# A feed-forward block's up-projections in pairs, by seven products of half size

## The chip, the cores and the metric

The kernel runs on one core of a Trainium2 chip. The metric is device microseconds of one execution: the median of three runs is 2164.41 us (2162.79 to 2165.35). TensorE (PE) multiplies into eight PSUM banks; VectorE (DVE), ScalarE (ACT) and GpSimd (POOL) do the elementwise work; SyncE (SP) issues the transfers.

## The reference, cut to what matters

One decoder layer on x of 1024 tokens by 1024 channels, all in float32: four token mixers, a cross-attention, and the feed-forward block. Each ends in `x <- LayerNorm(ALPHA * x + y)`. What is touched is the last:

```python
def _swiglu(x, w1, w3, w2):          # w1, w3: 1024 x 2816, w2: 2816 x 1024
    return (jax.nn.silu(x @ w1) * (x @ w3)) @ w2
x = _layer_norm(ALPHA * x + _swiglu(x, w1, w3, w2), ln_g[2], ln_b[2])
```

## The kernel before

**Products in three passes.** Every float32 operand is split into a high part (rounded, a copy on ACT) and a low part (the rest, a subtraction, on DVE or POOL): `split`, L153. A product is then three matmuls (`mm3`, L165): high by high for all slices of the sum, then low by high and high by low. `weight` (L157) loads 128 x 1024 numbers (512 KB) and splits them; raw, high and low tiles have two buffers each.

**The feed-forward stage.** The stream lies transposed: eight tiles x2 of 128 channels by 1024 tokens. The 2816 hidden channels are 22 blocks of 128. Of a block, `ffn_up` (L1427) makes w1 and w3 products for a half of 512 tokens: 24 matmuls each of 128x512 (8 slices of the sum, three passes). silu (ACT), the product with the w3 result (DVE) and a split give the tiles hh and hl. `ffn_down` (L1445) multiplies one block's 128 hidden channels by w2 for 8 output tiles and 2 halves: 3 matmuls into a PSUM bank, and one DVE addition into x2, 16 per block (L1459).

**Order.** The program is written out in one order; a scheduler then fixes each engine's own order from it, and each engine works its list in that order. First (LEAD = 3) blocks 0 to 2 for the first half of the tokens, while `Norm.steps` of the layer norm before runs for the second half beside them; `sink2` (L1407) splits each finished tile into the x2A (first half) or x2B (second half) operands, and POOL scales x2 by ALPHA. Then blocks 2 to 0 for the second half, their down-projections, and blocks 3 to 17 one by one, up and down in turn. The last four blocks (TAIL = 4) go by slices of 512, 256 and 256 tokens: all four blocks up, then down for that slice, weights loaded anew for each. A slice's norm (`Norm`: sum over eight tiles, mean matmul ps_mean, eight centred squares and their sum lnq, variance matmul ps_vc, a short DVE/ACT chain, broadcast matmul ps_rs, eight multiplications and affine steps) is laid beside the next slice's products; its matmuls stand at fixed places in PE's list (`queued`, L181). `LastNorm` does the last slice's.

Of the kernel before, what the change touches and what calls it, by code (L numbers as in the profile page):

```python
# [54 lines left out]
for _name, _w in (("ident", 128), ("bones", 128), ("ones256", 128), ("ones1k", 128), ("gce", 256),  # L55
                  ("tri", 128), ("id2", 64), ("ce", 256)):
    CC[_name] = _n
    _n += _w
# [34 lines left out]
def hybrid_kernel(ctx, tc, io, out):  # L93
# [12 lines left out]
    stg = ctx.enter_context(tc.tile_pool(name="stg", bufs=3))  # L106
    dp = ctx.enter_context(tc.tile_pool(name="dp", bufs=1, space=DRAM))
# [28 lines left out]
    def load_consts():  # L136
        nc.sync.dma_start(cst, io["consts"][:, 0:CC["ce"]])
# [1158 lines left out]

    def attend(hf, h):

        def scores(i):
# [6 lines left out]
            pr = t4.tile([P, MEM], F32, tag="xp", name="xp", bufs=2)  # L1306
# [114 lines left out]

    hid = {}

    def ffn_weights(f, e1=nc.vector, e3=nc.vector, **kw):
        return weight(io["ffn_w1"][f], eng=e1, **kw), weight(io["ffn_w3"][f], eng=e3)

    def ffn_up(f, sls, ws, steps=(0, 0)):  # L1427

        if f not in hid:
            hid[f] = tuple(pM.tile([P, T], F32R, tag="M", name=n) for n in ("hh", "hl"))  # L1430
        hh, hl = hid[f]
        for sl in sls:
            hf, n = sl.start // TH, sl.stop - sl.start
# [11 lines left out]
    def ffn_down(fs, ws, sls, ln=None):  # L1445
# [7 lines left out]
        for j0 in range(0, KD, 2):  # L1453
# [153 lines left out]
```

## Time and profile before

| what | value |
|---|---|
| median of three runs | 2164.41 us |
| the profiled execution | 2169.53 us, span 2167.4 us |
| granted TensorE clock, mean | 0.986 |
| PE busy | 2127.2 us (98%) |
| DVE / ACT / POOL busy | 1148.7 (53%) / 724.2 (33%) / 210.2 us (10%) |
| DMA | 161.12 MB, mean 74 GB/s |
| feed-forward stage | 1388.8 us to the end |

The page shows PE as busy nearly throughout, in matmuls that overlap (one of 128x512 is shown as 0.39 us, though the next begins 0.23 us later). So the busy share is no measure of the rate: count matmuls in a stretch instead. The windows of the rows below cut the stage at its own borders: the first blocks, the long middle, and three slices.

### The profile page before, as it was taken

To read this page: it belongs to the slowest core of one execution; us is meant where nothing else is said; L and a number is where in the kernel's file an instruction comes from. 1 tells how busy PE (TensorE), PEld (TensorE's weight loads), DVE (VectorE), ACT (ScalarE), POOL (GpSimd) and SP (SyncE) were. 2 spreads that over 40 slices of the span, in tenths; PEclk is the share of its full clock that TensorE was granted. 3 is DMA by queue.
4 is the path that set the end of the run, shared out by engine and by line. 5 is a ranking of instruction groups with operands and counts; after the bars stand their busy time and mean duration, and the time that the engine had idled before them with its cause. 6 is when DMAs were issued, how large, how long until landed. Compare 5 with 4: busy or idle time off the path is not lost. (4 is left out here: it accounts for less than half of the span.)

```text
span 2167.4 us, 29103 instructions
## 1 busy us (share of the span) xinstructions
PE 2127.2 (98%) x11884; PEld 1746.4 (81%) x11884; DVE 1148.7 (53%) x2028; ACT 724.2 (33%) x1163; POOL 210.2 (10%) x173
## 2 busy tenths in 40 slices
PE   9999999999999999999999999999999999999997
PEld 7877877787888888888897888778888888888787
DVE  5365498434544343334575446755554544545577
ACT  3243212266466564223243333331111111111224
POOL 0000000000001111211032000440000000000122
PEclk9999999999999999999999999999999999999999
DMA  6123221223211111113342112321111111111411
GB/s 212 49 70 88 72 87 61 88 78 102 76 61 60 49 52 47 53 47 109 111 160 97 31 58 88 127 65 52 59 49 39 59 49 40 59 49 59 146 69 49
DMA packets 87684, 161.12 MB, mean 74 GB/s; under 512 B 19606, under 2 KB 43848, under 8 KB 87552
## 3 DMA queue, kind: packets, MB, share of 16 engines
q1 hardware_dynamic: 87552, 159.28, 22.8%
q8 instruction: 93, 1.52, 0.3%
q14 instruction: 39, 0.32, 0.0%
HBM read 134.50 MB, written 24.76 MB: 73 GB/s over the span
## 5 line engine op out<-in xcount | busy, mean ns | idle before, releaser
L154 ACT CAST whi<-wraw 128x1024 fp32r<-128x1024 f32 x189 | 198.0, 1049 | 336.8 <-issue 192.8
L155 DVE TENSOR_TENSOR wlo<-wraw,whi 128x1024 fp32r<-128x1024 f32 x164 | 215.2, 1313 | 167.6 <-ACT whi L154 167.5
L176 PE MATMUL ps_gate<-xl,whi 128*128 128x512 f32 x512 | 201.5, 394 | 0.0
L175 PE MATMUL ps_gate<-xh,wlo 128*128 128x512 f32 x512 | 201.3, 393 | 0.0
L1459 DVE TENSOR_TENSOR x<-x,ps_w 128x512 f32<-128x512 f32 (+1 forms) x306 | 189.1, 673 | 11.8 <-PE ps_w L176 11.4
L172 PE MATMUL ps_gate<-xh,whi 128*128 128x512 f32 x512 | 165.6, 402 | 0.0
L175 PE MATMUL ps_g<-xh,wlo 128*128 128x512 f32 x400 | 157.8, 395 | 0.0
L176 PE MATMUL ps_g<-xl,whi 128*128 128x512 f32 x400 | 157.7, 394 | 0.0
L175 PE MATMUL ps_w<-x2B,wlo 128*128 128x512 f32 (+1 forms) x416 | 147.5, 365 | 3.6 <-POOL wlo L155 3.5
L176 PE MATMUL ps_w<-x2B,whi 128*128 128x512 f32 (+1 forms) x416 | 147.1, 364 | 0.0
L176 PE MATMUL ps_w<-hl,whi 128*128 128x512 f32 (+1 forms) x384 | 141.5, 374 | 1.9 <-DVE hl L155 1.7
L172 PE MATMUL ps_g<-xh,whi 128*128 128x512 f32 x400 | 140.4, 416 | 2.2 <-ACT xh L154 2.2
L175 PE MATMUL ps_w<-hh,wlo 128*128 128x512 f32 (+1 forms) x384 | 141.2, 373 | 0.0
L155 POOL TENSOR_TENSOR wlo<-wraw,whi 128x1024 fp32r<-128x1024 f32 x25 | 63.2, 2530 | 778.3 <-ACT whi L154 772.3
L175 PE MATMUL ps_w<-x2A,wlo 128*128 128x512 f32 x352 | 137.4, 390 | 0.0
L176 PE MATMUL ps_w<-x2A,whi 128*128 128x512 f32 x352 | 137.2, 390 | 0.0
L172 PE MATMUL ps_w<-hh,whi 128*128 128x512 f32 (+1 forms) x384 | 134.2, 375 | 2.1 <-ACT hh L154 2.1
L1442 DVE TENSOR_TENSOR hs<-hs,ps_w 128x512 f32<-128x512 f32 (+1 forms) x48 | 30.8, 642 | 177.5 <-PE ps_w L176 177.3
L176 PEld LDWEIGHTS ps_gate<-xl,whi 128*128 128x128 f32 x512 | 96.8, 189 | 20.7 <-issue 0.2
L175 PEld LDWEIGHTS ps_gate<-xh,wlo 128*128 128x128 f32 x512 | 96.7, 189 | 20.6 <-issue 0.2
L172 PEld LDWEIGHTS ps_gate<-xh,whi 128*128 128x128 f32 x512 | 94.7, 190 | 19.4 <-issue 1.9
L1050 POOL TENSOR_TENSOR merged<-merged,gsig 128x512 f32<-128x512 f32 x48 | 66.5, 1385 | 399.2 <-DVE gsig L1049 289.5
(457 smaller groups left out, 4259.6 us busy)
## 6 DMA issues: line engine op xcount, KB each, us to landing
wraw<-ffn_w SPq DMA_DIRECT2D x84, 512.0 KB
wraw<-wblk SPq DMA_DIRECT2D x57, 512.0 KB
wraw<-xa_wo SPq DMA_DIRECT2D x16, 512.0 KB
xraw<-xT SPq DMA_DIRECT2D x16, 256.0 KB
yld<-y_d SPq DMA_DIRECT2D x16, 256.0 KB
uraw<-ups SPq DMA_DIRECT2D x32, 128.0 KB
wraw<-w_out SPq DMA_DIRECT2D x8, 512.0 KB
xr<-xT SPq DMA_DIRECT2D x16, 256.0 KB
```

The source lines that it names most:

```text
L154: nc.scalar.copy(hi, src)
L155: eng.tensor_tensor(out=lo, in0=src, in1=hi.bitcast(F32), op=ALU.subtract)
L172: mm(ps, lhsT=pairs[i][0], rhs=pairs[i][2], start=start and i == 0, stop=False)
L175: mm(ps, lhsT=ll, rhs=rh, start=False, stop=False)
L176: latest[0] = mm(ps, lhsT=lh, rhs=rl, start=False, stop=stop and i == n + min(lag, n) - 1)
L1050: nc.gpsimd.tensor_tensor(out=mj, in0=mj, in1=sg, op=ALU.add)
L1442: tt(out=s, in0=s, in1=p[1], op=ALU.mult)
L1459: tt(out=x2[j][:, sl], in0=x2[j][:, sl], in1=ps, op=ALU.add)
```

## The change

Blocks 0 to 3 (LEAD = 4) are made as before, for one half at a time. Blocks 4 to 21 are taken as nine pairs. For a pair, w1 is a matrix of 256 by 1024: two block rows by two halves of the sum; x is two halves of the channels by two halves of the tokens. The product of two 2 x 2 block matrices takes eight half-sized products, or, by Strassen's scheme in Winograd's form, seven, of sums of blocks. `seven` (new) does this for w1 and then for w3: each of seven products is 12 matmuls of 128x512 (4 slices, three passes), against 96 matmuls for the same part before; four weight sums (POOL, `comb`), and seven sums of results (DVE). The sums of x are made once: eight in `sink2`, on POOL, beside the first blocks (xT12, xT3), and xT4 after them. Weights come as pieces of 128 x 2 x 512 (high and low together), each split by ACT and DVE, kept in a ring of five (`top_up`); raw rows are loaded one unit ahead. `down` sums a pair's two blocks in PSUM (6 matmuls, 8 DVE additions per block); the ALPHA scaling goes into the first of these additions. The last four blocks' slices (and of blocks 16 and 17 the second half's) hold only down-projections, with six w2 rows kept in SBUF; the norms of the first two slices add their sums on POOL instead of DVE. Constants that later stages don't need get a pool that closes before the last stages, which gives two more buffers.

```diff
     def sink2(hf):
         def f(j, ap):
             split(xf[hf].h[j], xf[hf].l[j], ap)
-            nc.gpsimd.tensor_scalar(out=ap, in0=ap, scalar1=ALPHA, scalar2=0.0, op0=ALU.mult, op1=ALU.add)
+            if hf == 1 and j >= KD // 2:
+                if not xt:
+                    xt.extend((HL(pA, "A", "xT12"), HL(t4, "T", "xT3", KD // 2)))
+                k = j - KD // 2
+                b11, b12 = (x2[k][:, hs(i)] for i in range(2))
+                t1 = diff(b12, b11)
+                split(xt[0].h[k], xt[0].l[k], t1)
+                t2 = diff(ap, t1)
+                split(xt[0].h[j], xt[0].l[j], t2)
+                t3 = diff(ap, b12)
+                split(xt[1].h[k], xt[1].l[k], t3)
...
-    LEAD, TAIL = 3, 4
+    LEAD = 4
...
+    RING = ((pB, "B"), (wp, "whi"), (wp, "wlo"), (wp, "whi"), (wp, "wlo"))
...
+    def sums(raws):
+        a11, a21, a22 = raws[0][:, 0:TH], raws[1][:, 0:TH], raws[1][:, TH:]
+        s1 = comb(a21, a22, ALU.add)
+        s2 = comb(s1, a11, ALU.subtract)
+        return s1, s2, comb(a11, a21, ALU.subtract)
...
+            s1, s2, s3 = ss
+            a = [r[:, i * TH:(i + 1) * TH] for r in raws for i in range(2)]
+            yield piece(a[0])
+            if more:
+                nxt = rows(units[u + 1], u + 1)
+            for src in (a[1], s2, s1, s3, a[3]):
+                yield piece(src)
+            s4 = comb(a[1], s2, ALU.subtract)
+            t = piece(s4)
+            ss = sums(nxt) if more and units[u + 1][0] != "ffn_w2" else None
+            yield t
...
+    def down(f, hfs, first=False):
+        for jh in range(2):
+            top_up(1)
+            w = made[used[0]:used[0] + 2]
+            for j in range(HK):
+                cs = slice(j * P, (j + 1) * P)
+                for hf in hfs:
+                    ps = gps("ps_w2")
+                    mm3(ps, [(w[i][:, 0, cs], w[i][:, 1, cs], hid[f + i, hf][:, 0], hid[f + i, hf][:, 1])
+                             for i in range(2)])
...
+        def product(n):
+            top_up()
+            ps = alloc()
+            w, (h, l) = made[used[0]], b[n]
+            mm3(ps, [(w[:, 0, k * P:(k + 1) * P], w[:, 1, k * P:(k + 1) * P], h[k], l[k]) for k in range(HK)])
+            used[0] += 1
...
+        u = term()
+        nc.scalar.copy(u, product(0))
+        done(0, 0, u, product(1))
+        tt(out=u, in0=u, in1=product(2), op=ALU.add)
+        v = term()
+        tt(out=v, in0=u, in1=product(3), op=ALU.add)
+        ps = product(4)
+        tt(out=u, in0=u, in1=ps, op=ALU.add)
+        done(1, 1, v, ps)
+        done(1, 0, u, product(5))
+        done(0, 1, v, product(6))
...
+        def hidden(i, l, a, ps):
+            x = t4.tile([P, TH], F32, tag="xp", name="hs", bufs=1)
+            tt(out=x, in0=a, in1=ps, op=ALU.add)
+            tt(out=x, in0=x, in1=gate[i, l], op=ALU.mult)
+            t = hid_tile(f + i, l, *((t4, "T") if lastp else ()))
+            split(t[:, 0], t[:, 1], x)
+
+        seven(lambda: sps("ps_w1"), rhs, gate_of)
+        if LEAD < f < NFF - 2:
+            down(f - 2, (0,) if f == NFF - 4 else (0, 1))
...
+        seven(lambda: gps("ps_w3"), rhs, hidden, keep)
...
+        ln = Norm(x2, sl, 2, gps, nc.gpsimd) if n < 2 else LastNorm(x2, sl, 2, gps)
```

What stands where, first on POOL in the first blocks (x2 tiles 0 to 7 end in 18 to 25 before and in 25 to 32 after; wlo is a weight's low part, the last two those of block 3). Before, behind the second half's multiplications:

```order
L1136 TENSOR_SCALAR x2_9718<-x2_9718,par_80 128x512
L1136 TENSOR_SCALAR x2_9719<-x2_9719,par_80 128x512
L1136 TENSOR_SCALAR x2_9720<-x2_9720,par_80 128x512
L1410 TENSOR_SCALAR x2_9718<-x2_9718 128x512
L1410 TENSOR_SCALAR x2_9719<-x2_9719 128x512
L1136 TENSOR_SCALAR x2_9721<-x2_9721,par_80 128x512
L1410 TENSOR_SCALAR x2_9720<-x2_9720 128x512
L1136 TENSOR_SCALAR x2_9722<-x2_9722,par_80 128x512
L1410 TENSOR_SCALAR x2_9721<-x2_9721 128x512
```

After:

```order
L1422 TENSOR_TENSOR xdiff_11849<-x2_9729,x2_9725 128x512
L1144 TENSOR_SCALAR x2_9730<-x2_9730,par_84 128x512
L162 TENSOR_TENSOR wlo_11910<-wraw_11907,whi_11909 128x1024
L1144 TENSOR_SCALAR x2_9731<-x2_9731,par_84 128x512
L1144 TENSOR_SCALAR x2_9732<-x2_9732,par_84 128x512
L1422 TENSOR_TENSOR xdiff_11857<-x2_9726 128x512
L1422 TENSOR_TENSOR xdiff_11861<-x2_9730,xdiff_11857 128x512
L1422 TENSOR_TENSOR xdiff_11865<-x2_9730,x2_9726 128x512
L1422 TENSOR_TENSOR xdiff_11873<-x2_9727 128x512
L1422 TENSOR_TENSOR xdiff_11877<-x2_9731,xdiff_11873 128x512
L1422 TENSOR_TENSOR xdiff_11881<-x2_9731,x2_9727 128x512
L162 TENSOR_TENSOR wlo_11916<-wraw_11913,whi_11915 128x1024
```

Short scalings of one input have given way to differences of two inputs, and the low parts of a fourth block's weights, 1024 wide, now stand among and behind them.

Second, on DVE in the middle. Before, where one block's up-projection ends and its predecessor's down-projection begins (hl is a hidden tile's low part):

```order
L155 TENSOR_TENSOR wlo_14059<-wraw_14056,whi_14058 128x1024
L1442 TENSOR_TENSOR hs_14051<-hs_14051,ps_w3_14026 128x512
L1459 TENSOR_TENSOR x2_9718<-x2_9718,ps_w2_14062 128x512
L155 TENSOR_TENSOR wlo_14145<-wraw_14142,whi_14144 128x1024
L155 TENSOR_TENSOR hl_13945<-hs_14051,hh_13944 128x512
L1459 TENSOR_TENSOR x2_9718<-x2_9718,ps_w2_14063 128x512
L1459 TENSOR_TENSOR x2_9719<-x2_9719,ps_w2_14064 128x512
```

After, in the w3 part of a pair, behind the fifth of its seven products (piece is a weight piece's low part, hid a hidden tile's):

```order
L1594 TENSOR_TENSOR term_13580<-term_13580,ps_w3_13673 128x512
L1654 TENSOR_TENSOR hs_13687<-term_13648,ps_w3_13673 128x512
L162 TENSOR_TENSOR piece_13693<-wcomb_13630,piece_13693 128x512
L1655 TENSOR_TENSOR hs_13687<-hs_13687,ps_w1_13381 128x512
L162 TENSOR_TENSOR hid_13690<-hs_13687,hid_13690 128x512
L162 TENSOR_TENSOR piece_13715<-wcomb_13628,piece_13715 128x512
L1654 TENSOR_TENSOR hs_13709<-term_13580,ps_w3_13696 128x512
L1655 TENSOR_TENSOR hs_13709<-hs_13709,ps_w1_13400 128x512
L162 TENSOR_TENSOR piece_13738<-wcomb_13632,piece_13738 128x512
L162 TENSOR_TENSOR hid_13712<-hs_13709,hid_13712 128x512
L1654 TENSOR_TENSOR hs_13731<-term_13648,ps_w3_13718 128x512
L1655 TENSOR_TENSOR hs_13731<-hs_13731,ps_w1_13418 128x512
```

The additions into x2 have moved to a part of their own; here the result sums, hidden tiles and pieces of the next unit alternate, each behind one that waits for ACT.

Third, on PE in the last slices, around the variance matmuls of the first slice's norm. Before, between two up-projections of the second slice:

```order
L175 MATMUL ps_w1_16087<-x2B_11217,wlo_16078 128x256
L176 MATMUL ps_w1_16087<-x2B_11221,whi_16077 128x256
L245 MATMUL ps_vc_16112<-cst_78,lnq_15973 128x1 x4
L176 MATMUL ps_w3_16125<-x2B_11218,whi_16083 128x256
L175 MATMUL ps_w3_16125<-x2B_11215,wlo_16084 128x256
L176 MATMUL ps_w3_16125<-x2B_11219,whi_16083 128x256
```

After:

```order
L183 MATMUL ps_w2_16428<-hid_15806,piece_16058 128x256
L182 MATMUL ps_w2_16428<-hid_16148,piece_16081 128x256
L252 MATMUL ps_vc_16404<-cst_81,lnq_16318 128x1 x4
L183 MATMUL ps_w2_16428<-hid_16148,piece_16081 128x256
L182 MATMUL ps_w2_16428<-hid_16110,piece_16089 128x256
L183 MATMUL ps_w2_16428<-hid_16110,piece_16089 128x256
```

They now stand in the second slice's fifth group of down-projections, 87 matmuls of 128x256 behind the slice's start; before, 137 such matmuls of the slice stood ahead of them.

## Rows read from the trace of the kernel before

**Rows 1.** The page's first part: busy us (share of the span) and instructions.
```profile
PE 2127.2 (98%) x11884; PEld 1746.4 (81%) x11884; DVE 1148.7 (53%) x2028; ACT 724.2 (33%) x1163; POOL 210.2 (10%) x173
```

**Rows 2.** Windows, all engines: stretches of the feed-forward stage; the first row names columns.
```profile
core 0: us, PE busy (x) PEld busy (x) DVE busy (x) ACT busy (x) POOL busy (x), PEclk, DMA share, GB/s
1425.10:1474.00 48.90, 46.45 (x196) 37.28 (x195) 24.16 (x29) 16.16 (x23) 16.92 (x17) 0.97 0.20 62
1474.00:2041.50 567.50, 566.52 (x2498) 467.40 (x2496) 291.81 (x410) 99.23 (x128) 9.58 (x4) 1.00 0.16 54
2041.50:2068.30 26.80, 23.94 (x98) 19.01 (x97) 14.35 (x17) 2.60 (x4) 2.35 (x1) 0.94 0.43 157
2068.30:2153.00 84.70, 79.39 (x607) 76.46 (x605) 65.45 (x121) 32.65 (x56) 26.94 (x22) 0.96 0.18 63
2153.00:2167.40 14.40, 4.03 (x24) 3.50 (x24) 7.42 (x26) 4.99 (x10) 2.23 (x4) 0.70 0.21 73
```

**Rows 3.** Timeline of PE at 2068: start, duration (us), line, op, tiles, shape, count.
```profile
2068.29 1.11 PE L172 MATMUL ps_w<-x2B,whi 128*128 128x256 f32 x8
2071.16 1.02 PE L1142 MATMUL ps_mean<-lns,cst 128*128 128x512 f32 x2
```

**Rows 4.** DVE, ACT groups by form: tiles, shape, count | busy us, mean ns | idle, releaser.
```profile
L1459 DVE TENSOR_TENSOR x<-x,ps_w 128x512 f32<-128x512 f32 x294 | 184.1, 683 | 9.0 <-PE ps_w L176 8.9
L155 DVE TENSOR_TENSOR xl<-xraw,xh 128x512 fp32r<-128x512 f32 x16 | 10.6, 690 | 1.3 <-ACT xh L154 1.3
L155 DVE TENSOR_TENSOR x2B<-x,x2B 128x512 fp32r<-128x512 f32 x8 | 7.4, 943 | 2.7 <-ACT x2B L154 2.6
L154 ACT CAST hh<-hs 128x512 fp32r<-128x512 f32 x40 | 24.7, 617 | 85.8 <-DVE hs L1442 85.8
```

**Rows 5.** POOL by line, L1050 and L1136: count, duration ns min/median/max, first and last start.
```profile
L1050 POOL TENSOR_TENSOR merged<-merged,gsig x48: 1271/1293/2210, 636.0 to 1013.6; 128x512 f32<-128x512 f32 x48
L1136 POOL TENSOR_SCALAR x<-x,par x48: 557/776/2768, 1089.3 to 2142.9; 128x512 f32<-128x512 f32 x40, 128x256 f32<-128x256 f32 x8
```

**Rows 6.** Timelines of DVE and POOL at 2080 and 2122: the same DVE operation twice.
```profile
2080.05 0.41 DVE L155 TENSOR_TENSOR hl<-hs,hh 128x256 fp32r<-128x256 f32 x1
2121.73 2.40 POOL L155 TENSOR_TENSOR wlo<-wraw,whi 128x1024 fp32r<-128x1024 f32 x1 [13.52 <-ACT whi L154]
2122.10 2.32 DVE L155 TENSOR_TENSOR hl<-hs,hh 128x256 fp32r<-128x256 f32 x1
```

**Rows 7.** The chain that ended last: start, us, what, around 2034 a weight's landing.
```profile
2034.42 4.64 DMA wraw<-ffn_w
```

**Rows 8.** Timelines of PE and POOL, 1425 to 1445; in brackets idle before and releaser.
```profile
1425.14 2.09 PE L172 MATMUL ps_w<-x2A,whi 128*128 128x512 f32 x8
1441.16 0.50 PE L172 MATMUL ps_w<-x2B,whi 128*128 128x512 f32 x1 [1.71 <-ACT x2B L154]
1425.70 2.40 POOL L155 TENSOR_TENSOR wlo<-wraw,whi 128x1024 fp32r<-128x1024 f32 x1 [4.57 <-ACT whi L154]
1428.09 3.23 POOL L1136 TENSOR_SCALAR x<-x,par 128x512 f32<-128x512 f32 x3
```

**Rows 9.** Timeline of PE at 2049: after a wait.
```profile
2049.33 0.74 PE L176 MATMUL ps_w<-hl,whi 128*128 128x512 f32 x1 [1.73 <-DVE hl L155]
2050.30 0.63 PE L175 MATMUL ps_w<-hh,wlo 128*128 128x512 f32 x1
2052.85 0.40 PE L175 MATMUL ps_w<-hh,wlo 128*128 128x512 f32 x1
```

**Rows 10.** Timeline of DVE in the last norms, and ACT's square by form.
```profile
2072.22 2.48 DVE L1121 TENSOR_TENSOR x<-x,ps_mean 128x512 f32<-128x512 f32 x4 [2.32 <-PE ps_mean L1142]
L1123 ACT ACTIVATE lnq<-x 128x512 f32<-128x512 f32 x40 | 24.7, 632 | 25.5 <-DVE x L1121 19.5 <-DVE lnq L1127 6.0
2152.97 0.42 DVE L1459 TENSOR_TENSOR x<-x,ps_w 128x256 f32<-128x256 f32 x1
2138.36 2.41 DVE L1132 TENSOR_TENSOR x<-x,ps_rs 128x256 f32<-128x256 f32 x7
```

More of the change, by code (lines that the diff above doesn't have):

```diff
@@ new lines, in hybrid_kernel, with piece, rows @@
+    RING = ((pB, "B"), (wp, "whi"), (wp, "wlo"), (wp, "whi"), (wp, "wlo"))
+    made, used = [], [0]
+    def piece(src, place=None, eng=nc.vector):
+        pool, tag = place or RING[len(made) % len(RING)]
+        t = pool.tile([P, 2, TH], F32R, tag=tag, name="piece")
+        split(t[:, 0], t[:, 1], src, eng)
+        return t
+    def rows(n, u):
+        pool, tag = (pM, "M") if u > 1 and u % 2 == 0 else (wp, "raw")
+        raws = []
+        for i in range(2):
+            raws.append(pool.tile([P, D], F32, tag=tag, name="wraw"))
+            nc.sync.dma_start(raws[i], io[n[0]][n[1] + i])
+        return raws
@@ new lines, in making @@
+    def making():
+        nxt, ss = rows(units[0], 0), None
+        for u, (n, f) in enumerate(units):
+            raws = nxt
+            more = u + 1 < len(units)
+            if n == "ffn_w2":
+                for i in range(4):
+                    yield piece(raws[i % 2][:, i // 2 * TH:i // 2 * TH + TH])
+                    if i == (3 if u < 2 else 0):
+                        nxt = rows(units[u + 1], u + 1)
+                if ss is None and units[u + 1][0] != "ffn_w2":
+                    ss = sums(nxt)
+                continue
+            s1, s2, s3 = ss
+            a = [r[:, i * TH:(i + 1) * TH] for r in raws for i in range(2)]
+            yield piece(a[0])
+            if more:
+                nxt = rows(units[u + 1], u + 1)
+            for src in (a[1], s2, s1, s3, a[3]):
[4 more added lines that the diff above has]
+            yield t
@@ new lines, in hybrid_kernel, with top_up @@
+    maker = making()
+    def top_up(n=99):
+        while n > 0 and len(made) - used[0] < len(RING):
+            t = next(maker, None)
+            if t is None:
+                return
+            made.append(t)
+            n -= 1
+    def down(f, hfs, first=False):
[8 more added lines that the diff above has]
+                             for i in range(2)])
+                    xs = x2[HK * jh + j][:, hs(hf)]
+                    if first:
+                        stt(out=xs, in0=xs, scalar=ALPHA, in1=ps, op0=ALU.mult, op1=ALU.add)
+                    else:
+                        tt(out=xs, in0=xs, in1=ps, op=ALU.add)
+                if j < HK - 1:
+                    top_up(1)
+            used[0] += 2
@@ L1481, in hybrid_kernel @@
[L1481 to L1485 removed]
+        g = lead_up(f, 1, w13[f] if f == LEAD - 1 else ffn_weights(f))
+        if f == 0:
+            top_up(1)
+            next(g)
+            top_up(2)
+        drain(g)
+    xt4 = HL(pA, "A", "xT4", HK)
+    for k in range(HK):
+        t = diff(x2[k + HK][:, hs(0)], xt[0].h[k + HK].bitcast(F32))
+        nc.gpsimd.tensor_tensor(out=t, in0=t, in1=xt[0].l[k + HK].bitcast(F32), op=ALU.subtract)
+        split(xt4.h[k], xt4.l[k], t)
```

197 lines of the change are left out of this document (117 added, 80 removed).

## Prediction

> **What bounds the kernel now.** I read four views, in this order. The page's first part: PE is busy 98% of the span, no other engine above 53% [rows 1]. The windows of the feed-forward stage, cut at its borders: in the long middle 2498 matmuls fill 567.5 us, 0.2272 us each for 128x512, at full granted clock, while DVE works 292 us and POOL 10 [rows 2]. So the middle goes at PE's rate and at nothing else's. The timeline of PE gives the narrow matmul: 24 of 128x256 between 2068.29 and 2071.16, 0.1196 us each [rows 3]. Last, for each other stretch, its length less its matmuls at these rates; the code gives the counts. First blocks (192 matmuls): 48.9 − 43.6 = 5.3 us. Middle (2496 by the code): 0.4. First slice (96): 26.8 − 21.8 = 5.0. Second and third (576 narrow): 84.7 − 68.9 = 15.8. Behind them 14.4 us pass with 24 matmuls. Losses before the end are thus 26.5 us; the reader is to see that they lie where norms and freshly loaded weights meet PE.
>
> The profiled execution took 2169.5 us (span 2167.4), 5.1 above the median of 2164.4. I work out a difference on the former and apply it to the latter. What a measurement of this kernel can tell from no change is 0.2%, 4.3 us.
>
> **What goes on PE.** From 1425.1 on the kernel before issues 192 + 2496 + 96 = 2784 wide and 576 narrow matmuls. After: 288 in the first blocks (the rest of blocks 2 and 3 for the first half, four for the second); in the middle 192 for their down-projections, 18 × 84 for nine pairs by seven products, 624 for later down-projections, 2328 together; 96 in the first slice; 288 narrow ones in the two others (six blocks, down alone). That is 2712 and 288. Cut: 72 × 0.2272 + 288 × 0.1196 = 16.4 + 34.4 = 50.8 us. On PE nothing hides this; the question is how much comes back as waits.
>
> **First blocks: loss 16 us (5.3 before).** Nine differences of x and the splits of their 24 results now pass through POOL, ACT and DVE beside blocks 0 to 3, and POOL makes the low parts of block 3's weights behind them. PE wants the low part of block 3's w3 behind 48 products of block 2, 24 of block 3's w1 and the 8 of the high-by-high pass: 1425.1 + 80 × 0.2272 = 1443.3. POOL begins the second half's affine steps at 1428.1 [rows 8]. Till that low part it does eight of them at 0.776 and nine two-input operations at 1.293, the merges' price [rows 5], and two low parts at 2.40 [rows 8]: 6.2 + 11.6 + 4.8 = 22.6, so 1450.7, a wait of 7.4 us. That is without waits for others. But a DVE operation with two SBUF inputs took 0.41 us alone and 2.32 beside POOL's 2.40 us subtraction, ending with it [rows 6]; the x2B splits average 0.943 against 0.690 for a like operation elsewhere [rows 4]. If all 15 of DVE's splits in this stretch exclude POOL, 15 × 0.69 = 10.4 us more: a wait of 17.8. I take 14, nearer the upper end, because the x2B row shows the holding at work in this very place. After a wait PE works at its 1.2 GHz level for a while: behind the 1.73 us at 2049 it spends 3.5 us at 0.63 a matmul before 0.40 returns [rows 9], half of it lost, 1.8. The 1.71 us wait for x2B [rows 8] and its like go, since x2B is split long before PE comes to it. 14 + 1.8 + 0.3 = 16; bounds 9.5 and 19.9.
>
> By the Trainium skill, page "SBUF — State Buffer", section "Who interferes with whom", a DVE instruction with two SBUF inputs and a GpSimd instruction that reads SBUF contend, and the lock is held for the instruction's length. The trace agrees with 0.41 and 2.32 us. Followed to its end the rule gives the 17.8, not the 7.4, and it speaks against the change wherever POOL is given more.
>
> **Middle: loss 2 us (0.4 before).** A pair has 168 matmuls up and 96 down: 264 × 0.2272 = 60.0 us, against 65.4 for what did its work before. Beside them DVE has 22 splits with two SBUF inputs (14 pieces' low parts of up-weights, four of w2, four hidden tiles) at 0.690 and 34 operations on PSUM at 0.683 [rows 4]: 15.2 + 23.2 = 38.4. POOL has eight sums of weights at 1.293 [rows 5]: 10.3. Even if the two exclude each other throughout, 48.7 of 60. ACT: 28 copies, splits and silus at 0.617 [rows 4], 17.3. None of them is a bound over a pair. Within a pair the w3 part is the tightest: 22 DVE operations, 15.1, and if four of POOL's sums fall there and exclude it, 20.3, against 84 × 0.2272 = 19.1 on PE. But pieces are made four products ahead, 4 × 12 × 0.2272 = 10.9 us, and the w1 part with 14 operations (9.6 us) lets DVE catch up. Result sums free four PSUM banks as before. A weight lands 4.64 us after its issue [rows 7]; behind it three sums on POOL, 3.9; 8.5 against 13.6 that five products and a bank's start give. Six rows of 512 KB in 60 us are 52 GB/s, as the middle's 54 before [rows 2]. So I take 2 us for nine pairs' seams and the middle's last one; bounds 0 and 11 (1.2 a pair for nine pairs, all of the w3 part's excess).
>
> **Slices: loss 14.5 us (20.8 before).** First slice: its weights are in SBUF, so the 5.0 us (1.73 at 2049 among them [rows 9]) go; 0.5, bounds 0 and 5. Then 87 narrow matmuls and the mean's, 10.9 us, stand ahead of the variance's. Its chain: mean 0.5, DVE's centring from about 3 us on at 0.6 each (2.48 for four [rows 10]), ACT's squares at 0.632 [rows 10], the eight squares summed on POOL, seven times 1.293 [rows 5], together with three half-width sums of the next slice's mean (estimated 0.73 each, half of 1.293 and a little): 11.2 us from about 6 on, 17.2. PE waits 6.3, and 1.8 at half clock behind it. The next slice's mean waits some 1.9 behind POOL's eight affine steps, and the norms' own matmuls take about 4 as before. Sum 14.0. If POOL is held off by DVE's affine multiplications and splits too, 20; if centring, squares and sums run abreast, 4.
>
> **End: 2.2 us more.** Before, DVE's seven multiplications by the broadcast of the second slice's norm (2.41, some 0.35 apart [rows 10]) lay well ahead of its last addition at 2152.97 [rows 10]. After, eight of them, 2.8 us, stand between the last slice's additions with nine matmuls, 1.1, to follow. 1.7 + 0.5; bounds 0 and 3. What comes behind stays at 14.4.
>
> **Ahead of the stage** the order differs by scalings of x that POOL no longer does and by constants loaded in two parts. I cost that at nothing: POOL is busy 10% there [rows 1], and the loads lie behind those of x; uncovered it would be one landing, 4.64 us [rows 7].
>
> **Sum.** Losses 16 + 2 + 14.5 + 2.2 = 34.7 against 26.5 before, +8.2; matmuls −50.8; net −42.6. 2164.4 − 42.6 = 2121.8: I predict 2122 us. With all low ends (9.5 + 0 + 4 + 0) it is 2101, with all high (19.9 + 11 + 25 + 3) 2146.
>
> **Rivals.** *POOL hides its work.* The lead's wait stays at 7.4 (9.5 with the clock) and the slices' sums run abreast of the centring (5): 9.5 + 2 + 5 + 1 = 17.5, 2105. For it: POOL is idle 90% of the span. Against it: the held instruction [rows 6] and four operations of 1.27 us or more, where 0.68 on DVE stood. Chance 15%.
>
> *DVE is late once in each pair.* The w3 part's 1.2 us of excess becomes a wait there, with 1.8 of half clock: 9 × 3.0 = 27 for 2, so 2147. For it: hidden tiles and pieces of the next unit stand alternately in DVE's list, each behind a copy on ACT. Against it: pieces are four products ahead. Chance 16%.
>
> *POOL's sums hold up DVE, and the kernel is slower.* All eight sums of a pair fall into one w3 part, and DVE's operations, those on PSUM too, wait behind them: 15.1 + 10.3 = 25.4 us against 19.1. Over nine pairs 9 × 6.3 = 57 us come back: 2164.4 − 42.6 − 2 + 57 = 2177 us. It decides from (42.6 + 2)/9 = 5.0 us a pair on. For it: in [rows 6] DVE lost 1.9 us to one POOL instruction, and the merges took up to 2.21 in place of 1.27 [rows 5], so both engines lose by it. Against it: half of the sums stand with the w1 part, and the holding shows in rows for an operation with two SBUF inputs only. Chance 6%.
>
> **How the numbers follow.** Forecast 63%, POOL hidden 15%, late DVE 16%, held DVE 6%. The forecast's own range from its bounds is 2105 to 2142. For 8 in 10 I let it reach both neighbours in part: 2104 to 2146. Faster by over 0.2% (below 2160): the forecast, the first two rivals, less a little of their tails, 0.92; within 0.2%, between the late and the held DVE, 0.03; slower 0.05.
>
> **What would show it.** Matmul records should fall by about 360, nearly all behind 1425. In the windows: the first blocks at 288 × 0.2272 + 16 = 81 us, the middle's 2328 matmuls in 531, the first slice in 22, the two others in 34.4 + 14 = 48. In the first blocks PE's longest wait should end on POOL's low part of block 3's w3; in the slices on POOL's sum of squares ahead of the variance. A middle at over 0.230 us a matmul, with PE's waits ending on DVE's pieces, would make the prediction wrong upward, and the mean of a piece's subtraction (0.69 or well over 1) tells which of the two rivals; a first stretch under 75 us downward.

## The result, and the profile after

The changed kernel takes 2129.2 us (median of four, 2126.6 to 2133.6) against 2164.9 in the same comparison: a ratio of 0.9836 with an interval of 0.9814 to 0.9858, 35.7 us faster. I had predicted 2122, in 2104 to 2146. The direction and the range held, and 7 of the 42.6 us that I had forecast did not come. The profiled execution took 2127.5 us, span 2125.7.

The page's first part, to be held against [rows 1]:

```profile
PE 2073.9 (98%) x11524; PEld 1700.1 (80%) x11524; DVE 1181.6 (56%) x2083; ACT 771.5 (36%) x1289; POOL 350.9 (17%) x280
```

360 matmul records fewer, the number that the code gives. PE is busy 98% again, so the page alone tells nothing of where the time went. The windows of the stage, cut at the same borders as [rows 2] (and ahead of them blocks 0 and 1 for the first half); columns as there:

```profile
1384.70:1418.70 34.00, 31.04 (x134) 24.93 (x135) 21.88 (x30) 15.00 (x20) 13.19 (x5) 0.95 0.29 93
1418.70:1501.60 82.90, 71.42 (x292) 57.41 (x291) 51.82 (x52) 30.43 (x47) 46.65 (x30) 0.92 0.20 64
1501.60:2031.90 530.30, 527.91 (x2329) 436.96 (x2328) 339.34 (x493) 151.47 (x257) 113.71 (x82) 1.00 0.17 57
2031.90:2053.70 21.80, 21.80 (x97) 18.04 (x97) 7.75 (x12) 3.33 (x6) 12.73 (x10) 1.00 0.00 1
2053.70:2109.80 56.10, 45.70 (x320) 44.50 (x319) 28.98 (x72) 12.74 (x26) 26.63 (x31) 0.85 0.10 38
2109.80:2125.70 15.90, 4.13 (x26) 3.32 (x24) 8.93 (x31) 3.40 (x8) 6.46 (x12) 0.67 0.39 133
```

Row by row: blocks 0 and 1 (before 1388.8 to 1425.1) take 34.0 in place of 36.3. From block 2 on the first blocks take 82.9, with 288 x 0.2272 = 65.4 of matmuls: 17.5 lost, where I had put 16. The middle has 530.3 (531 forecast), the first slice 21.8 (22.3), the end 15.9 (14.4 before, 16.6 forecast). The last two slices have 56.1, where 34.4 + 14 = 48.4 was forecast: 21.7 lost. That is the one row that is far off. The longest causes of PE's waits in the first blocks, the middle and the slices (us in total, times, longest):

```profile
PE ps_vc L252 <- POOL lnq L1135: 8.8, 2, 5.8
PE ps_lead L182 <- POOL wlo L162: 6.2, 2, 4.8
PE ps_lead L179 <- ACT whi L161: 6.0, 2, 5.3
PE ps_w L179 <- ACT hid L161: 2.4, 1, 2.4
PE ps_mean L1150 <- POOL lns L1124: 1.6, 1, 1.6
```

They are waits for POOL, or for an ACT operation that stands behind POOL's work. The first three and the last lie in the first blocks and in the last slices (but for 0.7 of the third, at the stage's start). The one of 2.4 is the only one in the middle: its first down-projection, at 1505.9, waits for a cast that stands in ACT's list behind one of a POOL difference for xT4. PE also waits for DVE in blocks 0 and 1 (3.0) and in the end (1.8 and 2.5); before, the like places had 3.0 and 2.6.

### The profile page after: what moved, and what is told of

Read it like the earlier page. It is cut to its first block, busy times and chain, and to the rows that moved or that the text cites. A ratio compares the mean times of both kernels' runs of the same rounds, so it can differ in the third digit from the quotient of the medians.

```text
span 2125.7 us, 28942 instructions
## 1 busy us (share of the span) xinstructions
PE 2073.9 (98%) x11524; PEld 1700.1 (80%) x11524; DVE 1181.6 (56%) x2083; ACT 771.5 (36%) x1289; POOL 350.9 (17%) x280
## 4 chain that ended last, share of the span: by engine, by line
PE 92%; POOL 3%; DVE 2%; ACT 1%; issue 1%; DMA 1%; SPq 0%; DVEq 0%; POOLq 0%; ACTq 0%
PE ps_w L179 9%; PE ps_w L183 9%; PE ps_w L182 9%; PE ps_gate L179 6%; PE ps_gate L183 5%; PE ps_gate L182 5%; PE ps_g L179 5%; PE ps_g L183 4%; PE ps_g L182 4%; PE ps_q L182 3%; PE ps_q L183 3%; PE ps_q L179 2%; PE ps_up L179 1%; PE ps_up L182 1%; PE ps_up L183 1%; PE ps_wo L183 1%
## 5 line engine op out<-in xcount | busy, mean ns | idle before, releaser
L162 DVE TENSOR_TENSOR wlo<-wraw,whi 128x1024 fp32r<-128x1024 f32 x103 | 140.9, 1368 | 65.9 <-ACT whi L161 65.7
L161 ACT CAST whi<-wraw 128x1024 fp32r<-128x1024 f32 x119 | 124.7, 1049 | 72.1 <-issue 19.3
L183 PE MATMUL ps_w<-hid,piece 128*128 128x512 f32 (+1 forms) x400 | 145.0, 370 | 0.0
L182 PE MATMUL ps_w<-hid,piece 128*128 128x512 f32 (+1 forms) x400 | 144.6, 369 | 0.0
L161 ACT CAST piece<-wraw 128x512 fp32r<-128x512 f32 x102 | 62.6, 623 | 170.4 <-PE ps_w L183 163.6
L1566 DVE TENSOR_TENSOR x<-x,ps_w 128x512 f32<-128x512 f32 x120 | 82.5, 688 | 65.1 <-PE ps_w L183 65.0
L179 PE MATMUL ps_w<-hid,piece 128*128 128x512 f32 (+1 forms) x400 | 110.3, 371 | 2.4 <-ACT hid L161 2.4
L182 PE MATMUL ps_w<-xT,piece 128*128 128x512 f32 x288 | 112.0, 389 | 0.0
L183 PE MATMUL ps_w<-xT,piece 128*128 128x512 f32 x288 | 112.0, 389 | 0.0
L1056 DVE TENSOR_TENSOR gsig<-gsig,ps_up 128x512 f32<-128x512 f32 x48 | 33.0, 688 | 132.0 <-PE ps_up L183 113.4
L161 ACT CAST piece<-wcomb 128x512 fp32r<-128x512 f32 x72 | 44.0, 622 | 135.2 <-PE ps_w L183 135.2
L1051 ACT ACTIVATE gsig<-ps_gate,par 128x512 f32<-128x512 f32 x64 | 44.1, 689 | 132.2 <-PE ps_gate L183 131.7
```

The lines of the kernel that those rows point to most:

```text
L161: nc.scalar.copy(hi, src)
L162: eng.tensor_tensor(out=lo, in0=src, in1=hi.bitcast(F32), op=ALU.subtract)
L179: mm(ps, lhsT=pairs[i][0], rhs=pairs[i][2], start=start and i == 0, stop=False)
L182: mm(ps, lhsT=ll, rhs=rh, start=False, stop=False)
L183: latest[0] = mm(ps, lhsT=lh, rhs=rl, start=False, stop=stop and i == n + min(lag, n) - 1)
L1051: act(sg, ps, AF.Sigmoid, bias=pc("gateb", br * 8 + j))
```

## Experiments

All comparisons below are medians. The changed kernel's 2128.9 comes from the comparison that also has the first two runs on DVE; the later runs are held against it, though the kernel before, which stands in every comparison, moves between 2165.7 and 2167.9 from one to the next. Window rows have the columns of [rows 2].

**The two kernels again.** No edit.

> The changed kernel once more, to see how far its stretches repeat. Theory: the loss sits in the same two places, so the windows repeat: 17.5 us lost in the first blocks (82.9 us from block 2's first product, 288 matmuls), 1 to 2 in the middle, 21.8 in the last two slices; 2127 to 2131 us. Rival: the differences between executions lie in these waits themselves, and one of the three stretches differs by over 3 us.

2128.9 us, ratio 0.9834 (0.9820 to 0.9848). First blocks from block 2 on, and the last two slices:

```profile
1420.20:1502.90 82.70, 72.78 (x291) 58.44 (x290) 51.70 (x52) 30.41 (x47) 46.56 (x30) 0.90 0.20 64
2055.10:2111.10 56.00, 45.65 (x320) 44.45 (x319) 28.95 (x72) 12.72 (x26) 26.55 (x31) 0.85 0.10 38
```

They repeat to 0.2 us.

> The kernel before once more. Its profiled execution was 5 us above its median, and in the changed kernel the feed-forward stage began 4.1 us earlier (1384.7 against 1388.8). Theory: that is the one execution, not the change; here the stage begins at 1384 to 1386. Rival: the change itself (constants in two parts, no scalings on POOL) gives 4 us ahead of the stage; then it begins at 1388 to 1390 again.

The stage began at 1389.3, the rival's number. But over the twelve profiles of kernels with the change it began between 1383.2 and 1390.6, 1386.1 on average: what one execution shows ahead of the stage varies by more than the 4.1 us in question, so a gain of some 3 us there is likely and not shown. Blocks 0 and 1 of before:

```profile
1389.30:1425.60 36.30, 32.66 (x133) 26.00 (x134) 22.58 (x30) 13.54 (x19) 13.91 (x7) 0.91 0.27 89
```

36.3 for blocks 0 and 1 repeats, so the 2.3 us gained there are the change's. But from block 2 on the first blocks take 46.4 and the last two slices 82.9, which is 2.5 and 1.8 us less than in [rows 2], at a granted clock of 1.00 and 0.98 in place of 0.97 and 0.96: before's own losses vary by as much, so a stretch of that kernel can't be read to a tenth of a microsecond. From block 2 on, the two kernels differ by 742.3 − 707.0 = 35.3 us in the first profiles and 739.4 − 706.8 = 32.6 in the second.

**The norms' sums on DVE.**

```diff
-        ln = Norm(x2, sl, 2, gps, nc.gpsimd) if n < 2 else LastNorm(x2, sl, 2, gps)
+        ln = Norm(x2, sl, 2, gps) if n < 2 else LastNorm(x2, sl, 2, gps)
```

> The norms of the first two slices add their sums on DVE, as before the change, not on POOL. Theory: POOL's 1.29 us a step (with the next slice's sums between) makes PE wait 5.8 + 1.6 + 3.0 us for the two variances and a mean, and each long wait costs some 3 us at the lower clock behind it. On DVE a step of centring and sum takes 0.62 + 0.68 and nothing else on POOL is in the way: the first wait falls to 1 to 3 us, the others to under 1. The two slices lose 10 to 14 us in place of 21.8; 8 to 11 us faster than the changed kernel. Rival: the additions into x2 stand in DVE's list behind the norm's sums, so PE's banks come free late, and the time moves by less than 3 us either way.

2114.5 us, 14.4 below the changed kernel. The last two slices and the end:

```profile
2056.00:2094.10 38.10, 38.10 (x311) 37.40 (x309) 32.68 (x80) 10.78 (x21) 6.03 (x8) 1.00 0.15 56
2094.10:2113.70 19.60, 7.90 (x34) 6.35 (x32) 12.39 (x45) 5.26 (x14) 6.53 (x12) 0.57 0.32 108
```

The slices lose 3.7 us in place of 21.7, more than the theory gave, and the end gives 3.7 back: DVE's fuller list finishes the second norm later. No wait stands before the first variance any more, and the second norm's now stands behind the slices' last product, at 2094.90. Is it DVE's speed that took the first wait away? Mean and variance of the first norm on PE and the last sum of its squares, first here, then the mean and the last sum of the changed kernel, whose variance came at 2070.92:

```profile
2058.82 1.02 PE L1150 MATMUL ps_mean<-lns,cst 128*128 128x512 f32 x2
2071.55 0.95 PE L252 MATMUL ps_vc<-cst,lnq 128*128 128x1 f32 x8
2070.28 0.69 DVE L1135 TENSOR_TENSOR lnq<-lnq 128x512 f32<-128x512 f32 x1
```

```profile
2056.58 1.02 PE L1150 MATMUL ps_mean<-lns,cst 128*128 128x512 f32 x2
2069.61 1.26 POOL L1135 TENSOR_TENSOR lnq<-lnq 128x512 f32<-128x512 f32 x1
```

From the mean to the end of the sum 12.2 us here and 14.3 there: speed gives 2.1 of the 5.8. The rest is place: 123 narrow matmuls now stand ahead of the variance, not 87, as the scheduler put it later in PE's list with sums of another engine: 36 x 0.12 = 4.3 us. PE came to it 12.7 us behind the mean here, and 8.6 there. By these times speed alone would have left a wait of some 3.6 us and place alone one of 1.6; no run changed one without the other. So my theory had the right engine, and the smaller half of the mechanism.

**The differences of x on DVE.**

```diff
-        nc.gpsimd.tensor_tensor(out=t, in0=a, in1=b, op=ALU.subtract)
+        nc.vector.tensor_tensor(out=t, in0=a, in1=b, op=ALU.subtract)
...
-        nc.gpsimd.tensor_tensor(out=t, in0=t, in1=xt[0].l[k + HK].bitcast(F32), op=ALU.subtract)
+        nc.vector.tensor_tensor(out=t, in0=t, in1=xt[0].l[k + HK].bitcast(F32), op=ALU.subtract)
```

> The differences of x (12 in the first blocks, 8 for xT4) on DVE in place of POOL. Theory: POOL's list is what PE waits for in the first blocks (4.8 for block 3's w1 low part, 5.3 for a cast that stands in ACT's list behind casts of POOL's differences, 1.4 for w3's low part), and POOL and DVE hold each other up besides; on DVE the 20 differences take 0.69 each, 13.8 us, without the holding. The first blocks lose 6 to 10 us in place of 17.5; 7 to 11 us faster. Rival: the 20 operations only move the delay into DVE's list, where splits, norm and hidden tiles wait behind them: the loss stays within 3 us of 17.5.

2117.6 us, 11.3 below. (`sink2` makes 12 differences, not the eight that the section on the change names; xT4 takes eight more.) The first blocks, and PE's longer waits in them:

```profile
1419.40:1493.20 73.80, 67.97 (x290) 54.88 (x290) 52.27 (x71) 30.02 (x47) 19.25 (x11) 0.98 0.22 71
```

```profile
1432.61 0.50 PE L182 MATMUL ps_lead<-x2A,wlo 128*128 128x512 f32 x1 [0.27 <-POOL wlo L162]
1449.75 0.80 PE L179 MATMUL ps_lead<-x2B,whi 128*128 128x512 f32 x1 [3.96 <-ACT x2B L161]
```

8.4 lost in place of 17.5, as the theory gave: POOL's low parts come within a microsecond, and the wait for w3's cast falls from 5.30 to 0.91. A new wait of 4.0 for x2B appears, since ACT's casts and DVE's splits of x2B stand behind those of the differences (tested below). The middle's head no longer waits, either: 528.0 in place of 530.3.

**Sums of weights on DVE, and twice on POOL.**

```diff
-        nc.gpsimd.tensor_tensor(out=t, in0=a, in1=b, op=op)
+        nc.vector.tensor_tensor(out=t, in0=a, in1=b, op=op)
```

> The 72 sums of weight blocks in the middle on DVE in place of POOL. Theory: the middle has slack on every engine but PE; DVE gets 8 x 0.69 = 5.5 us a pair more, 43.9 of 60, and still makes its pieces four products ahead: within 3 us of the changed kernel, the middle's 2328 matmuls again in 529 to 533 us. Rival (late DVE): the w3 part's 22 operations and four sums more, 17.9 us of 19.1, make PE wait for a piece once in each pair: 10 to 27 us slower, with PE's waits ending on DVE's pieces.

```diff
-        nc.gpsimd.tensor_tensor(out=t, in0=a, in1=b, op=op)
+        for _ in range(2):
+            nc.gpsimd.tensor_tensor(out=t, in0=a, in1=b, op=op)
```

> Each of the 72 sums of weight blocks is made twice on POOL, the same result into the same tile, so that POOL's share of the middle doubles. Theory: POOL's work there, 20.6 us in place of 10.3 of 60, and the holding of DVE, some 1 us for each operation that meets one, stay covered by pieces made ahead: 0 to 5 us slower. Rival (held DVE): DVE's 38.4 and POOL's 20.6 exclude each other, 59 of 60, and in the w3 part 15.1 + 10.3 and more against 19.1: 20 to 60 us slower, PE waiting for pieces in every pair.

2129.4 and 2129.3 us: no difference. The middle of the one and of the other:

```profile
1502.80:2033.20 530.40, 528.01 (x2330) 436.86 (x2328) 369.48 (x565) 151.37 (x257) 12.98 (x10) 1.00 0.17 57
```

```profile
1507.30:2037.70 530.40, 528.01 (x2329) 437.01 (x2329) 373.87 (x493) 150.53 (x257) 228.26 (x154) 1.00 0.16 57
```

530.4 both times, as in the changed kernel, with DVE at 369 or POOL at 228 us (339 and 114 before the edits). DVE's subtractions for pieces, from the instructions by tile (ns min/median/max), changed kernel first, then with each sum made twice:

```profile
L162 DVE TENSOR_TENSOR piece<-wraw,piece x90: 683/693/1531, 1493.7 to 2017.0; 128x512 fp32r<-128x512 f32 x90
```

```profile
L162 DVE TENSOR_TENSOR piece<-wraw,piece x90: 680/942/1824, 1499.5 to 2022.7; 128x512 fp32r<-128x512 f32 x90
```

The median subtraction goes from 0.693 to 0.942 us, since it now often meets a POOL operation, and PE doesn't feel it. Both rivals that cost time in the middle took the w3 part's excess, 1.2 or 6.3 us a pair, for a wait. With POOL's sums doubled that part has far more work than its 19.1 us if the two engines exclude each other, and no wait comes. That pieces are made four products ahead would explain it, and was not tested by itself; nor did a run find the load at which PE begins to wait.

**All eight products.**

```diff
-            s1, s2, s3 = ss
...
+            for src in a[1:]:
+                yield piece(src)
...
+    def eight(alloc, b, done, ready={}):
+        for i in range(2):
+            top_up()
+            w = made[used[0]:used[0] + 2]
+            for l in range(2):
+                ps = alloc()
+                mm3(ps, [(w[m][:, 0, k * P:(k + 1) * P], w[m][:, 1, k * P:(k + 1) * P], b[l][m][0][k], b[l][m][1][k])
+                         for m in range(2) for k in range(HK)])
...
+                done(i, l, ps)
```

> The nine pairs by all eight products, two of them summed in a PSUM bank, with pieces of the weights themselves: no sums of x, of weights or of results. Pairs, ring of pieces, down-projections by pairs, slices with w2 alone and the norms' sums on POOL stay. Theory: PE gets 18 x 12 matmuls of 128x512 more, 216 x 0.2272 = 49.1 us, and the first blocks lose 8 to 11 us less, since POOL has no differences to make: 2129 + 49 - 10 = 2168, 2163 to 2173 us, so all of the net gain against the kernel before comes from the seventh product left out, and the rest of the change gives and takes about the same. Rival: the seven products' sums cost PE time of their own in the middle that the eight don't have; then the middle grows by less than 44 us and the kernel by less than 30.

2161.6 us, ratio to before 0.9973 (0.9962 to 0.9984), 32.8 above the changed kernel and a little under the range that I gave. The profiled execution, at 2155.3, was the shortest of six. First blocks, middle, last two slices:

```profile
1418.10:1485.80 67.70, 66.32 (x291) 53.95 (x290) 31.85 (x37) 21.70 (x33) 15.54 (x11) 1.00 0.24 78
1485.80:2062.70 576.90, 576.90 (x2545) 477.51 (x2544) 210.24 (x313) 128.23 (x220) 10.55 (x8) 1.00 0.15 52
2084.50:2138.10 53.60, 43.25 (x319) 42.06 (x318) 28.90 (x72) 12.73 (x26) 26.59 (x31) 0.90 0.11 40
```

The middle is 46.6 us longer: 216 x 0.2272 = 49.1, less the wait of 2.4 at its head, which is gone. The first blocks lose 2.3 us (67.7 − 65.4) in place of 17.5: the differences of x on POOL cost 15.2 there, not the 8 to 11 that I had expected. So one product of eight left out brings 49.1 and the sums of x take back some 17.6, in the first blocks and at the middle's head. The rest of the change brings 4.2 us by the medians, about what can be told from nothing; on PE it trades 288 narrow matmuls for 144 wide ones, 34.4 against 32.7, and where the other 2.5 come from was not followed.

The last two slices are 2.5 us shorter than the changed kernel's 56.1, though nothing was edited there and PE waits as long at the same places: 5.72, 1.60 and 3.02 us. What differs is the clock, 0.90 in place of 0.85, and PE's busy time, 43.25 in place of 45.70. From PE's timeline, behind the two waits for a variance:

```profile
2101.65 1.86 PE L252 MATMUL ps_vc<-cst,lnq 128*128 128x1 f32 x8 [5.72 <-POOL lnq L1135]
2106.30 0.28 PE L182 MATMUL ps_w<-hid,piece 128*128 128x256 f32 x1
2131.66 0.61 PE L252 MATMUL ps_vc<-cst,lnq 128*128 128x1 f32 x4 [3.02 <-POOL lnq L1135]
```

Behind the first the 2.4 GHz level is back from 2106.3 on, 4.7 us after the wait; behind the second PE still works at it (0.12 us a matmul) until 2133.6, and falls to the lower level only then, until 2136.9. The changed kernel, as shown further on, is at the lower level for 7.0 and 6.7 us behind the same waits.

**Both parts on DVE, and later.**

> The norms' sums of the first two slices and the differences of x both on DVE. Theory: the two losses lie 550 us apart and add: 14.4 + 11.2 us faster than the changed kernel, 2103 (2101 to 2106). Rival: the execution differences seen so far (2 us) are in them twice, or DVE's longer list in the first blocks moves the middle: 2107 to 2112.

2105.6 us (2101.0 to 2106.0), 23.3 below the changed kernel, in the theory's range; the two add but for 2.4 us. First blocks:

```profile
1417.20:1492.40 75.20, 69.32 (x292) 55.84 (x291) 52.38 (x71) 30.20 (x48) 19.26 (x11) 0.95 0.21 70
```

They are 1.4 us longer than with the differences alone, with the same waits and at a clock of 0.95 in place of 0.98. The slices and the end take 38.1 and 19.0. Then the 12 differences are issued behind the blocks' second halves:

```diff
+              def later(j=j, ap=ap):
...
+              todo.append(later)
...
         drain(g)
+        todo[LEAD - 1 - f]()
```

> As with both parts on DVE, and the 12 differences with their splits are issued later: four portions, one behind each block's second half, not beside the splits of x2B. Theory: what is left in the first blocks (75.2 us from block 2 on for 65.4 of matmuls) is a list order: x2B's last splits stand behind differences in ACT's and DVE's lists (a wait of 4.0, and the lower clock behind it). With the differences behind them the stretch takes 66 to 69 us and the kernel 2097 to 2101. Rival: the 20 differences and 20 splits then meet the weights' low parts of blocks 2 to 0 and the first pieces on DVE, PE waits there or in the first pair, and the gain is under 2 us.

2099.6 us, ratio to before 0.9685 (0.9666 to 0.9704), the fastest of all, 29 below the changed kernel. First blocks, last two slices, end:

```profile
1420.30:1490.60 70.30, 66.66 (x292) 53.86 (x291) 52.33 (x71) 30.46 (x48) 16.20 (x11) 1.00 0.23 75
2040.30:2078.40 38.10, 38.10 (x311) 37.42 (x309) 32.65 (x80) 10.77 (x21) 6.03 (x8) 1.00 0.15 57
2078.40:2097.80 19.40, 7.53 (x34) 6.27 (x32) 12.30 (x46) 5.28 (x14) 6.52 (x12) 0.61 0.32 108
```

70.3 in the first blocks, 4.9 shorter, a little outside the 66 to 69 expected: the wait of 4.0 for x2B is gone, short ones for weights stay.

> The same late differences, but on POOL, with the norms' sums on DVE. It tells POOL's speed from the place in the list. Theory: in the 43.6 us of the second halves POOL has nothing else to do, 20 operations of 1.3 to 1.7 us fit, and PE waits in the first blocks as little as with DVE: 66 to 70 us from block 2 on, 2097 to 2103. Rival: POOL's slower operations and the holding of DVE's splits make the first pair or the first down-projections late; then the stretch and the head of the middle together lose over 6 us.

2113.5 us: the theory is wrong. The rival's loss of over 6 us came, but in the first blocks and not in the first pair. From block 2 on the first blocks take 81.5 us, nearly as with the early differences on POOL. The timelines of POOL and PE show why (start, us, then the operation; one of the twelve differences, and PE's longest wait):

```profile
1425.79 1.30 POOL L1422 TENSOR_TENSOR xdiff<-x 128x512 f32<-128x512 f32 x1
1467.41 3.78 PE L179 MATMUL ps_lead<-x2B,whi 128*128 128x512 f32 x8 [5.52 <-ACT whi L161]
```

The differences still run from 1425.8 on, among the affine steps, while block 3's second half, behind which the first of them stand in the code, begins at 1450.9: the scheduler pulled them forward in POOL's list. Place thus changed only in part, with four of them ahead of block 3's last low part where nine stood. PE's wait for the first of its low parts is 4.29 us (4.83 in the changed kernel), and that for a weight's cast comes back as 5.52 us, later, in the second halves. So this run does not tell speed from place. That POOL's list is what PE waits for stays shown by the run with DVE and by that without differences.

**Two mixtures for the slices**, both with late differences on DVE: squares' sums on DVE and sums for the mean on POOL; and the first norm on DVE, the second on POOL.

```diff
-            self.idx, self.alloc, self.eng = idx, alloc, eng
+            self.idx, self.alloc, self.eng, self.eng2 = idx, alloc, nc.vector, eng
...
-                self.eng.tensor_tensor(out=self.s, in0=a, in1=self.ap[j], op=ALU.add)
+                self.eng2.tensor_tensor(out=self.s, in0=a, in1=self.ap[j], op=ALU.add)
```

> Late differences on DVE; in the first two slices' norms the squares' sums on DVE and the sums for the mean on POOL. With all on DVE the two slices took 38.1 us and the end 19.0 (15.5 to 15.9 with POOL), since DVE's list is full in the last slice. Theory: taking 14 sums off DVE's list brings the last slice's norm forward: slices and end together 1 to 3 us shorter than 57.1. Rival: POOL's half-width sums hold DVE's sums of squares, and slices and end together are 57 to 61.

2101.9 us. Slices and end take 39.6 + 19.2 = 58.8 where 57.5 stood with all sums on DVE: the rival.

```diff
+        ln = Norm(x2, sl, 2, gps, (nc.vector, nc.gpsimd)[n]) if n < 2 else LastNorm(x2, sl, 2, gps)
```

> As with late differences on DVE; of the two slices' norms only the first one's sums are on DVE, the second one's on POOL as in the changed kernel. It tells the two waits for a variance apart. Theory: the first norm's wait (5.8, and some 3 behind it) and the mean's (1.6) stay away, the second's (3.0, and some 3 behind it) comes back: the two slices take 43 to 46 us (38.1 with both on DVE, 56.1 with both on POOL) and the end 15.5 to 16.5 in place of 19.4; 2101 to 2104. Rival: without the first norm's sums in its list POOL is early enough; then the slices take 38 to 40, and the kernel is 2 to 4 us below the one with both on DVE.

2102.1 us, the theory's number in each part, the two stretches and the wait for the second variance:

```profile
2041.60:2085.70 44.10, 39.84 (x315) 38.86 (x314) 32.28 (x77) 12.78 (x27) 17.61 (x22) 0.98 0.13 48
2085.70:2101.20 15.50, 5.14 (x30) 4.22 (x28) 9.84 (x33) 3.19 (x7) 6.52 (x12) 0.61 0.40 136
2082.15 0.61 PE L252 MATMUL ps_vc<-cst,lnq 128*128 128x1 f32 x4 [3.00 <-POOL lnq L1135]
```

44.1 and 15.5. So of the 18.0 us that the two slices lose with both norms on POOL, the second norm by itself makes 6.0, and 12.0 are left for the first, which was not run alone. The 6.0 are not the sum that I had expected, though. The mean's wait is the second norm's and came back too (1.26), and behind the 3.00 PE works at the 2.4 GHz level until 2083.7, so that the lower clock costs only about 1 us inside the slices. And 3.9 of the 6.0 are had back in the end, 15.5 in place of 19.4.

## Why the prediction was right, and where it was off

**Matmuls: right.** −360 records. The eight products confirm the rate at which I turned them into −50.8 us: 216 matmuls, 46.6 us and the 2.4 of the wait that went.

**First blocks: size near (17.5 for 16), in part by luck, and place half right.** I had one wait for the low part of block 3's w3, 14 us, and 1.8 of lower clock. The trace has three waits, 11.5 together, here with what ACT, POOL and DVE did meanwhile (start, us; in brackets the wait and its releaser):

```profile
1436.59 0.80 PE L182 MATMUL ps_lead<-x2A,wlo 128*128 128x512 f32 x1 [4.83 <-POOL wlo L162]
1447.15 3.78 PE L179 MATMUL ps_lead<-x2A,whi 128*128 128x512 f32 x8 [5.30 <-ACT whi L161]
1452.28 0.80 PE L182 MATMUL ps_lead<-x2A,wlo 128*128 128x512 f32 x1 [1.35 <-POOL wlo L162]
1445.53 0.62 ACT L161 CAST xT<-xdiff 128x512 fp32r<-128x512 f32 x1 [1.05 <-POOL xdiff L1422]
1446.06 1.04 ACT L161 CAST whi<-wraw 128x1024 fp32r<-128x1024 f32 x1
1439.49 1.29 POOL L1422 TENSOR_TENSOR xdiff<-x 128x512 f32<-128x512 f32 x1
1443.79 1.71 POOL L1422 TENSOR_TENSOR xdiff<-x 128x512 f32<-128x512 f32 x1
1437.01 0.68 DVE L162 TENSOR_TENSOR x2B<-x,x2B 128x512 fp32r<-128x512 f32 x1
1444.30 1.74 DVE L162 TENSOR_TENSOR x2B<-x,x2B 128x512 fp32r<-128x512 f32 x1
```

PE stops first at w1's low part, 4.83 us, because POOL's list had differences ahead of it already there. The 5.30 behind it end on ACT's cast for w3: an engine little more than a third busy (30.4 of 82.9), whose list holds casts of POOL's differences in front. I had followed POOL's list alone, and not the lists that stand still behind it, so the sign that I had named, the longest wait on POOL's low part of w3, did not come. What I had counted did: nine differences stand ahead of that low part, and PE gets it 33.6 us behind block 2's first product (1418.71 to 1452.28), for 18.2 of matmuls. The lower clock makes about 5 us, not 1.8: PE is busy 71.4 in this stretch, and 66.3 and 66.7 in the two runs that have it at a clock of 1.00 (the eight products, and the late differences on DVE). So a wait 2.5 too long and a clock 3 too short all but cancel. The holding that moved me to the upper value shows in both directions: DVE's split of x2B takes 0.68 at 1437.0 and 1.74 at 1444.3, where a POOL difference had begun before it, and POOL's difference 1.29 alone and 1.71 at 1443.8, where DVE had begun. In [rows 6] only DVE had lost.

**Middle: right.** 1.4 us lost for 2, and none of it by sums of weights or of results: it is the wait at the head, for a cast behind POOL's last differences of x. Both costly rivals fell with the two runs on the weights' sums.

**The last two slices: the step that failed is its size, 14.0 put, 21.7 measured.** By its parts: the first variance's wait 5.77 (6.3 put), the mean's 1.61 (1.9). Not in the sum at all was the second norm's variance, which waits for POOL in the same way: 3.02 us. And I took 1.8 us for the lower clock, from a wait of 1.73 [rows 9]. Around the wait of 5.77, and the one of 3.02:

```profile
2063.19 0.88 PE L179 MATMUL ps_w<-hid,piece 128*128 128x256 f32 x6
2070.92 1.87 PE L252 MATMUL ps_vc<-cst,lnq 128*128 128x1 f32 x8 [5.77 <-POOL lnq L1135]
2073.43 1.48 PE L179 MATMUL ps_w<-hid,piece 128*128 128x256 f32 x6
2101.90 1.02 PE L252 MATMUL ps_vc<-cst,lnq 128*128 128x1 f32 x4 [3.02 <-POOL lnq L1135]
```

Six high-by-high matmuls take 1.48 us at the 1.2 GHz level and 0.88 at 2.4, and the lower level lasts from 2070.9 to 2077.9. The 4.6 us of narrow matmuls from 2072.65 to 2077.27 at 0.213 in place of 0.120 lose 2.0, the eight variance matmuls 1.73 for 0.9, so about 3 us, and the second norm's wait is followed by the same (2101.9 to 2108.6). Waits 5.8 + 1.6 + 3.0 = 10.4, clock about 6, the norms' own matmuls and their seams the rest, about 5. So the 7.7 us that the prediction missed are the second variance with its clock, 6.0; 1.2 us more of clock behind the first; and 1.3 in the norms' own matmuls and seams; less 0.8 on the two waits that it had. The waits are read from PE's records and add up to its idle time, 56.1 − 45.7. The clock's 6 us are a size of this kernel, which repeats in its second profile (56.0), and not of the waits: the eight products have the same waits with 2.5 us less. Why was not tested.

By the Trainium skill, page "SBUF — State Buffer", section "Who interferes with whom", the lock falls to whichever of the two engines issues first and the other is blocked. The trace agrees with 1.74 and 1.71 us on the two sides. In the middle this cost nothing, even with POOL's work doubled.

**End: right in kind,** 1.5 us for 2.2: the eight multiplications by the broadcast stand on DVE ahead of the last slice's last addition, which comes at 2111.89.

```profile
2108.90 2.74 DVE L1140 TENSOR_TENSOR x<-x,ps_rs 128x256 f32<-128x256 f32 x8 [1.20 <-PE ps_rs L271]
```

**Ahead of the stage: wrong by a gain.** I cost it at nothing, and blocks 0 and 1 are 2.3 us shorter in all but one of the profiles with the change (34.0 or 34.1 in eleven, 35.2 in the first with the differences on DVE, against 36.3 twice). The trace shows where. Before, a product of another stage, ps_q, that stands among block 0's first matmuls waits for a weight's low part, and matmuls at the lower level follow: 8.3 us from block 0's first matmul to its sixth, against 6.0 after, where no wait stands between them. The kernel before:

```profile
1390.92 0.80 PE L175 MATMUL ps_q<-qB,wlo 128*128 128x512 f32 x1 [0.68 <-DVE wlo L155]
1391.94 0.63 PE L175 MATMUL ps_q<-qB,wlo 128*128 128x512 f32 x1
```

Just ahead of the stage, PE's wait for block 0's first weight is 0.66 us in place of 1.90. Why these weights are split sooner was not tested. In the profiled execution these 6.4 us (4.1 + 2.3) hid the miss in the slices: its difference is 41.7, near my 42.6, while the medians differ by 35.7.

## What to carry to other kernels

In this kernel trading products for sums paid in full where the sums had a long steady stretch to hide in, and cost most where it is set up: price the first use in every in-order list on the way to PE, not in the slowest engine's alone. Count each repetition of a wait (here two norms, not one), and give every long wait a price in clock behind it, as a range: behind the same 3.0 us it was about 3 us in one kernel here and between 1 and 2 in two others. Where work goes to a slower engine, look too at how much stands in PE's list ahead of what depends on it: of the 5.8 us at the first variance, speed took 2.1, and 36 matmuls more ahead of it covered the rest.

## What the runs showed of the hardware

- The holding between DVE and POOL goes both ways: 0.68 to 1.74 us for DVE's split, 1.29 to 1.71 for POOL's difference, in the same stretch.
- How long TensorE stays at its 1.2 GHz level behind a wait does not follow from the wait alone: behind 5.8 us it was 7.0 in the changed kernel and 4.7 with the eight products, and behind 3.0 it set in at once for 6.7 us or only after 2 us of matmuls at the 2.4 GHz level, for 3.3. Behind the 1.7 of [rows 9] it was 3.5.
- The first blocks and the last two slices repeat to 0.2 us in the two profiles of the changed kernel, and differ by 2.5 and 1.8 us in the two of the kernel before, where the shorter ones had the higher clock. The start of the stage varies by 7.4 us over the twelve profiles with the change; what varies ahead of it was not looked at.
